# First modulation matrix of a Hyena and DeltaNet trunk layer: 512 KB blocks that also use the weight slots, four quadrants of 256 columns per block

## The chip, the core and the metric

The kernel runs on one core of a Trainium2 chip. The metric is the device time of one execution in microseconds (us), as the median of the runs shown; smaller is better. Everything is float32 in memory. Products with large weights are made of three matmuls on split operands (a rounded high part and the rest).

## What is computed

One trunk layer acts on 128 context tokens and 256 latent tokens (T = 384) of width D = 2048. It consists of a half-step SwiGLU, a mixer (Hyena long convolutions beside a gated DeltaNet) and a second half-step SwiGLU. Each of the three is normalised before and after and modulated by shift, scale and gate vectors, which come out of a product of two conditioning vectors with the matrix `ada_w` (2048 x 18432). What the opening needs of it:

```python
def adaln(x, g, shift, scale):
    return rms_norm(x, g) * (1.0 + scale) + shift
...
    mod_ctx = (silu(c_ctx)[None] @ ada_w[l] + ada_b[l]).reshape(1, 1, N_MOD, D_MODEL)
    mod_lat = (silu(c) @ ada_w[l] + ada_b[l]).reshape(n_lat_req, 1, N_MOD, D_MODEL)
...
    h = adaln(x, norm_pre[0], mod[:, :, 0], mod[:, :, 1])
    x = x + 0.5 * mod[:, :, 2] * rms_norm(swiglu(h, ffn_wg[0], ffn_wu[0], ffn_wd[0]), norm_post[0])
```

So before the first large product can run, the first 4096 columns of `ada_w` (32 MB; shift and scale of the first sub-layer) have to be multiplied with two vectors, the tokens normalised, and `h` made. Beside this the kernel computes in its opening the spectra of the Hyena's long filters, which depend on the filter weights alone.

## The kernel before

A scheduler sets the order of the instructions on each engine when the program is built; each engine then runs its list in order, and waits where an instruction needs something that is not there yet. An instruction that waits holds up all behind it on its engine, and this includes DMA issues.

`run` (from line 1209) starts with an opening of some 150 us, which is written as two interleaved strands:

- `first_mods` (line 282) goes in two halves g over 16 row blocks kt of the matrix. Each step loads 1 MB of `ada_w` (L296, tile `aw`, three buffers, issued on SP's queue) and multiplies it on TensorE (PE) with the two conditioning vectors: four matmuls of 32 x 512 (L302), one for each quadrant of 32 columns of the array, into one PSUM bank `ada`. After each half come a copy (L307, ScalarE, called ACT), four transposes (L310) and the sums that give `modT` and `ab`. `modulate` then makes 8 of the 16 slices k of `h` (L431 on VectorE, called DVE; L433 on ACT), its rounded part `hh` (L123, ACT) and the rest `hl` (L124, here on GpSimd, called POOL).
- The generator `work` is advanced once per step. It holds the Hyena filters (`filters`) and, in `tokens`, the token work. The filters go through four turns, one for each order and half of the channels: matmuls L715/L716, windowed taps `fh` (L718), their sums in `slot` (L723/L724), absolute values `fab` (L726 to L728), norms (L733/L735), transforms by matmul (L745, L753), their copies and sums `fev` (L746, L754, L756, L757), and six stores `spec` of 256 KB to DRAM per turn (L740, issued on ACT's queue). The token work stands after the first turn: transposes of the tokens (L267, with L270 or L277), the squares (L406, ACT) with their sums on PE (L408), the root (L410 to L416), its spread (L445) and a copy of it (L1253).

`hl` lies in the buffer that `slot` held, so that the first write of `hl` comes after the last L753 that reads `slot`.

What follows, from the first `ffn` on, is dense work on PE: `unit` (line 128) loads 512 KB of weights (L142, SP), rounds them (`hi`, L123, ACT) and forms the rest (`lo`, L124, DVE), with three buffers each of `raw`, `hi` and `lo` of 512 KB in a pool `wp` of their own; `mm3` runs L149 to L151. `self.gate` holds the first weight loads back until some named instructions are done: the load of step kt = 12 of the first half, and two of the filters.

The DMA issues of SP and ACT together take eight completion semaphores (DMAHW0 to DMAHW7 in the orders below) in turn, in the scheduler's order; a load that takes one waits until the earlier load on it has landed.

Of the kernel before, what the change touches and what calls it, by code (L numbers as in the profile page):

```python
# [11 lines left out]
F32 = mybir.dt.float32  # L12
# [7 lines left out]
P = 128  # L20
D = 2048
KT = D // P
# [6 lines left out]
DH = 1024  # L29
# [76 lines left out]
class Builder:  # L106
# [175 lines left out]
    def first_mods(self, pool, x, hh, hl, work):  # L282

        nc = self.nc
        w = self.I["ada_w"][0][:, :2 * D].rearrange("r (m c) -> r m c", m=2)
        ab = pool.tile([P, 2, KT], F32, name="ab0")
        pre = self.vec["pre"]
        rb = None  # L290
        asb = self.early(512)
        for g in range(2):
            pa = self.psm.tile([P, 512], F32, tag="mm", name="ada")
            for kt in range(KT):
                aw = pool.tile([P, 2, DH], F32, tag="aw", name="aw", bufs=3)
                load = nc.sync.dma_start(out=aw, in_=w[kt * P:kt * P + P, :, g * DH:g * DH + DH])  # L296
                if g == 0 and kt == 12:
                    self.gate.append(load.ins)
                for m in range(2):
                    for h in range(2):  # L300
                        q = 32 * (2 * m + h)
                        nc.tensor.matmul(pa[q:q + 32, :], self.cs[:, kt, :], aw[:, m, h * 512:h * 512 + 512],  # L302
                                         start=kt == 0, stop=kt == KT - 1)
                got = next(work, None)
                rb = got if got is not None else rb
            sb = asb
            nc.scalar.copy(out=sb, in_=pa)  # L307
            pt = self.aux()
            for k in range(4):
                nc.tensor.transpose(pt[:, k * P:k * P + P], sb[:, k * P:k * P + P], self.ident)  # L310
            src = pt.rearrange("p (k m h v) -> p m h k v", k=4, m=2, h=2)
            gs = slice(8 * g, 8 * g + 8)
            b = self.vec["adab"][:, :2 * KT].rearrange("p (m t) -> p m t", m=2)[:, :, gs].rearrange("p m (h k) -> p m h k", h=2)
            for v in range(2):
                dst = self.modT[:, 0:2, v, gs].rearrange("p m (h k) -> p m h k", h=2)
                nc.vector.tensor_tensor(out=dst, in0=src[:, :, :, :, v], in1=b, op=ALU.add)
                nc.vector.scalar_tensor_tensor(out=ab[:, v, gs], in0=self.modT[:, 1, v, gs], scalar=1.0, in1=pre[:, gs],
                                               op0=ALU.add, op1=ALU.mult)
            for k in range(8 * g, 8 * g + 8):
                self.modulate(pool, 0, k, ab, x, rb, hh, hl, nc.gpsimd)  # L320
# [1060 lines left out]
```

## Time and profile before

| | us |
|---|---|
| median of 3 runs (lowest, highest) | 3302.22 (3301.97, 3307.99) |
| the profiled execution | 3302.25 |
| its span, first to last instruction | 3300.5 |
| PE busy in the span | 3200.0 (97%) |
| VectorE busy | 2091.5 (63%) |
| ScalarE busy | 1091.9 (33%) |
| GpSimd busy | 194.8 (6%) |
| mean granted TensorE clock, share of full speed | 0.987 |

The profile is of one execution. Its span is 1.75 us shorter than the time of the same execution, and that time lies within 0.03 us of the median. Times in rows count from the span's start. An engine is busy while an instruction runs on it; "idle before" and the waits name what released it. Rows with a q behind the engine (SPq, ACTq) are the DMA issues of that engine.

### The profile page before, as it was taken

What the parts mean: (1) busy time and instruction counts of PE and PEld (TensorE: products, weight loads), DVE (VectorE), ACT (ScalarE), POOL (GpSimd) and SP (SyncE); (2) the same over time, 40 slices, a digit from 0 to 9 for tenths busy, and PEclk for the clock granted to TensorE, in tenths of its full rate; (3) what the DMA queues carried; (4) which work ended last, traced back from release to release, by engine and by line L of the source; (5) the groups of instructions that cost most, each with busy time, mean ns of one, the idle gap of its engine ahead of it and who ended that gap; (6) DMA issues with size and microseconds to landing.
All of it is one profiled execution on the core that took longest, in us unless ns stands there. A gap on an engine that the chain in (4) does not pass through costs nothing.

```text
span 3300.5 us, 43912 instructions
## 1 busy us (share of the span) xinstructions
PE 3200.0 (97%) x17485; PEld 2915.9 (88%) x17485; DVE 2091.5 (63%) x2838; ACT 1091.9 (33%) x1583; POOL 194.8 (6%) x225
## 2 busy tenths in 40 slices
PE   6899999999999997999999999989999999999998
PEld 2499999899999996999999998879899999999996
DVE  4579889797979646677656665489444334444335
ACT  3442222222222235333333333353222222222223
POOL 1110000000000002000122320020000000000001
PEclk9899999999999998999999999989999999999999
DMA  9877767676868543433422234448343344333343
GB/s 331 281 264 253 235 224 249 211 240 218 258 211 257 166 153 126 140 125 114 123 75 67 77 96 160 131 142 264 122 150 125 128 128 126 124 127 125 125 130 113
DMA packets 362356, 554.03 MB, mean 168 GB/s; under 512 B 19876, under 2 KB 264970, under 8 KB 360360
## 3 DMA queue, kind: packets, MB, share of 16 engines
q1 hardware_dynamic: 351272, 527.59, 49.5%
q0 software_dynamic: 2800, 12.32, 1.1%
q10 hardware_dynamic: 8080, 11.33, 1.0%
q8 instruction: 137, 2.24, 0.3%
q14 instruction: 67, 0.55, 0.0%
HBM read 535.91 MB, written 15.25 MB: 167 GB/s over the span
## 4 chain that ended last, share of the span: by engine, by line
PE 88%; DVE 6%; DMA 3%; issue 2%; POOL 1%; ACT 1%; DVEq 0%; ACTq 0%; SPq 0%; POOLq 0%
PE mm L151 18%; PE mm L149 18%; PE mm L150 18%; PE mt L559 8%; PE mt L557 8%; PE mt L558 8%; DMA aw<-in_ada_w_dram 2%; DVE acc L339 1%; PE pb L1095 1%; PE pb L1090 1%; DVE lo L124 1%; PE aux L1137 1%; PE aux L1161 1%; PE ada L302 1%; PE pa L346 1%
## 5 line engine op out<-in xcount | busy, mean ns | idle before, releaser
L124 DVE TENSOR_TENSOR lo<-raw,hi 128x1024 fp32r<-128x1024 f32 (+1 forms) x676 | 823.6, 1220 | 714.6 <-ACT hi L123 712.9
L123 ACT CAST hi<-raw 128x1024 fp32r<-128x1024 f32 (+1 forms) x676 | 707.2, 1047 | 1616.9 <-PE mm L150 958.0
L150 PE MATMUL mm<-hl,hi 128*128 128x384 f32 x2320 | 779.6, 336 | 0.1
L149 PE MATMUL mm<-hh,hi 128*128 128x384 f32 x2320 | 776.4, 337 | 1.3 <-DVE hx L770 1.0
L151 PE MATMUL mm<-hh,lo 128*128 128x384 f32 x2320 | 765.1, 337 | 0.0
L339 DVE SCALAR_TENSOR_TENSOR acc<-aw,cs,acc 128x1024 f32<-128x1024 f32 x420 | 520.1, 1280 | 25.5 <-DMA aw<-in_ada_w_dram 24.5
L150 PE MATMUL mm<-yl,hi 128*128 128x384 f32 x1408 | 470.4, 334 | 0.0
L149 PE MATMUL mm<-yh,hi 128*128 128x384 f32 x1408 | 468.7, 334 | 0.7 <-ACT yh L123 0.7
L151 PE MATMUL mm<-yh,lo 128*128 128x384 f32 x1408 | 465.7, 334 | 1.4 <-DVE lo L124 1.4
L149 PEld LDWEIGHTS mm<-hh,hi 128*128 128x128 f32 x2320 | 434.1, 187 | 7.7 <-ACT hi L123 3.2
L150 PEld LDWEIGHTS mm<-hl,hi 128*128 128x128 f32 x2320 | 434.5, 187 | 6.9 <-issue 4.0
L151 PEld LDWEIGHTS mm<-hh,lo 128*128 128x128 f32 x2320 | 432.9, 187 | 8.0 <-issue 5.6
L558 PE MATMUL mt<-hi,gl 128*128 128x512 f32 x1056 | 414.1, 392 | 0.0
L557 PE MATMUL mt<-hi,gh 128*128 128x512 f32 x1056 | 413.5, 392 | 0.1
L559 PE MATMUL mt<-lo,gh 128*128 128x512 f32 x1056 | 398.8, 394 | 1.4 <-DVE lo L124 1.4
L149 PEld LDWEIGHTS mm<-yh,hi 128*128 128x128 f32 x1408 | 264.1, 188 | 1.5 <-ACT yh L123 1.1
L151 PEld LDWEIGHTS mm<-yh,lo 128*128 128x128 f32 x1408 | 263.9, 188 | 1.7 <-DVE lo L124 1.7
L150 PEld LDWEIGHTS mm<-yl,hi 128*128 128x128 f32 x1408 | 264.3, 188 | 0.4
L557 PEld LDWEIGHTS mt<-hi,gh 128*128 128x128 f32 x1056 | 198.2, 188 | 48.2 <-issue 3.4
L559 PEld LDWEIGHTS mt<-lo,gh 128*128 128x128 f32 x1056 | 198.2, 188 | 47.5 <-DVE lo L124 2.6
L558 PEld LDWEIGHTS mt<-hi,gl 128*128 128x128 f32 x1056 | 198.3, 188 | 44.6
L582 DVE TENSOR_TENSOR yacc<-mt,yacc 128x512 f32<-128x512 f32 x216 | 145.1, 687 | 145.1 <-PE mt L559 144.4
(344 smaller groups left out, 2455.5 us busy)
## 6 DMA issues: line engine op xcount, KB each, us to landing
aw<-in_ada_w_dram SPq DMA_DIRECT2D x224, 512.0 KB, 4.4
raw<-in_ffn_wg_dram SPq DMA_DIRECT2D x176, 512.0 KB, 3.8
raw<-in_ffn_wu_dram SPq DMA_DIRECT2D x176, 512.0 KB, 4.4
raw<-in_ffn_wd_dram SPq DMA_DIRECT2D x176, 512.0 KB, 3.5
raw<-in_w_in_dram SPq DMA_DIRECT2D x112, 512.0 KB, 3.6
aw<-in_ada_w_dram SPq DMA_DIRECT2D x32, 1024.0 KB, 8.2
raw<-in_w_out_dram SPq DMA_DIRECT2D x32, 512.0 KB, 3.7
spec<-fev ACTq DMA_DIRECT2D x24, 256.0 KB, 5.9
```

Of the source, the lines that this page charges most:

```text
L123: self.nc.scalar.copy(out=hi, in_=src)
L124: return (eng or self.nc.vector).tensor_tensor(out=lo, in0=src, in1=hi, op=ALU.subtract)
L149: t.matmul(out, hi[:, k, c], xh, start=first, stop=False)
L150: t.matmul(out, hi[:, k, c], xl, start=False, stop=False)
L151: t.matmul(out, lo[:, k, c], xh, start=False, stop=last)
L302: nc.tensor.matmul(pa[q:q + 32, :], self.cs[:, kt, :], aw[:, m, h * 512:h * 512 + 512], start=kt == 0, stop=kt == KT - 1)
L339: nc.vector.scalar_tensor_tensor(out=d, in0=aw, scalar=self.cs[:, kt, v:v + 1], in1=d, op0=ALU.mult, op1=ALU.add)
L346: nc.tensor.matmul(pa[32 * q:32 * q + 32, :], self.pick[:, v], acc[:, v, q * 512:q * 512 + 512], start=v == 0, stop=v == 1)
L557: mm(pts[t], xh[:, ts], hi[:, k], start=first, stop=False)
L558: mm(pts[t], xl[:, ts], hi[:, k], start=False, stop=False)
L559: mm(pts[t], xh[:, ts], lo[:, k], start=False, stop=last)
L582: nc.vector.tensor_tensor(out=y, in0=pt, in1=y, op=ALU.add)
```

## The change

The matrix comes in 64 blocks of 512 KB (one half m of the columns at a time) instead of 32 of 1 MB. Of every five of the first 46 blocks three take a slot of the pool `wp` (one of the nine of `raw`, `hi` and `lo`, in turn), the other two and all later ones take one of six buffers of their own (3 MB, as much as before). So up to 15 blocks can be ahead, then six. Each block is multiplied by four matmuls of 32 x 256, one per quadrant, and each m has a PSUM bank of its own; two copies bring both banks together, and the views of the transposed result are written for the new layout. The gate for the first sub-layer weights moves from the load of the 13th MB to that of block 52 (the 53rd, in the 27th MB).

```diff
+        spare = itertools.cycle(("raw", "hi", "lo"))
+        def block(i, src):
+            if i < 46 and i % 5 > 1:
+                aw = self.wp.tile([P, DH], F32, tag=next(spare), name="aw", bufs=3)
+            else:
+                aw = pool.tile([P, DH], F32, tag="aw", name="aw", bufs=6)
+            load = nc.sync.dma_start(out=aw, in_=src)
+            if i == 52:
+                self.gate.append(load.ins)
+            return aw
         for g in range(2):
-            pa = self.psm.tile([P, 512], F32, tag="mm", name="ada")
+            pa = [self.psm.tile([P, 512], F32, tag="mm", name="ada")[:, :256] for m in range(2)]
             for kt in range(KT):
-                aw = pool.tile([P, 2, DH], F32, tag="aw", name="aw", bufs=3)
-                load = nc.sync.dma_start(out=aw, in_=w[kt * P:kt * P + P, :, g * DH:g * DH + DH])
-                if g == 0 and kt == 12:
-                    self.gate.append(load.ins)
+                aw = [block((g * KT + kt) * 2 + m, w[kt * P:kt * P + P, m, g * DH:g * DH + DH]) for m in range(2)]
                 for m in range(2):
-                    for h in range(2):
-                        q = 32 * (2 * m + h)
-                        nc.tensor.matmul(pa[q:q + 32, :], self.cs[:, kt, :], aw[:, m, h * 512:h * 512 + 512],
-                                         start=kt == 0, stop=kt == KT - 1)
+                    for q in range(4):
+                        nc.tensor.matmul(pa[m][32 * q:32 * q + 32], self.cs[:, kt, :],
+                                         aw[m][:, q * 256:q * 256 + 256], start=kt == 0, stop=kt == KT - 1)
                 got = next(work, None)
                 rb = got if got is not None else rb
             sb = asb
-            nc.scalar.copy(out=sb, in_=pa)
+            for m in range(2):
+                nc.scalar.copy(out=sb[:, m * 256:m * 256 + 256], in_=pa[m])
```

In the kernel after, lines from `block` on are ten higher: the loads are L300, the block matmuls L311, the copies L317, the transposes L320, the squares L416, the stores `spec` L750, the last transforms L763; L142 and L149 to L151 keep their numbers. The scheduler sets a new order, and three places of it matter below.

First, ACT around the token work. Before, the four later stores of turn 0 stand ahead of the copies of the transposed tokens, and wait for semaphores of early loads and stores:

```order
L740 DMA spec<-fev 128x2x256 [waits DMAHW3_49,DVE_49]
L740 DMA spec<-fev 128x2x256 [waits DMAHW5_49]
L740 DMA spec<-fev 128x2x256 [waits DMAHW7_49,DVE_49]
L740 DMA spec<-fev 128x2x256 [waits DMAHW0_49]
L270 COPY x<-aux 128x4x128 [waits PE_49] x4
L406 ACTIVATE early<-x 128x384 [waits DVE_49,Activation_49]
```

After, on ACT:

```order
L270 COPY x<-aux 128x4x128 [waits PE_49] x4
L750 DMA spec<-fev 128x2x256 [waits DMAHW3_49,DVE_49]
L750 DMA spec<-fev 128x2x256 [waits DMAHW4_49]
L750 DMA spec<-fev 128x2x256 [waits DMAHW6_49,DVE_49]
L750 DMA spec<-fev 128x2x256 [waits DMAHW7_49]
L416 ACTIVATE early<-x 128x384 [waits DVE_49,Activation_49]
```

The stores now stand right ahead of the first square, and the semaphores that they take belong to blocks of the matrix. Which, SP's order shows, here blocks 33 to 41 (the first block is 0), on which the eight semaphores go round with the gaps that ACT's stores take:

```order
L300 DMA aw<-in_ada_w_dram 128x1024 [waits DMAHW4_49,PE_49]
L300 DMA aw<-in_ada_w_dram 128x1024 [waits DMAHW5_49,PE_49]
L300 DMA aw<-in_ada_w_dram 128x1024 [waits DMAHW6_49,PE_49]
L300 DMA aw<-in_ada_w_dram 128x1024 [waits DMAHW7_49,PE_49]
L300 DMA aw<-in_ada_w_dram 128x1024 [waits DMAHW0_49,PE_49]
L300 DMA aw<-in_ada_w_dram 128x1024 [waits DMAHW1_49,PE_49]
L300 DMA aw<-in_ada_w_dram 128x1024 [waits DMAHW2_49,PE_49]
L300 DMA aw<-in_ada_w_dram 128x1024 [waits DMAHW5_49,PE_49]
L300 DMA aw<-in_ada_w_dram 128x1024 [waits DMAHW0_49,PE_49]
```

Between the seventh and the ninth of these rows the stores took DMAHW3 and 4, then 6 and 7; the loads last on those are blocks 32, 33, 35 and 36.

Second, ACT in turn 2 of the filters. Before, from the absolute values of its first third to the first transform copy, with the rounding of the first weights (`hi`) long done in turn 1:

```order
L726 ACTIVATE fab<-fh 128x512 [waits DVE_49]
L701 CAST wf<-w_616 128x512 [waits DMASW2_49,DMASW1_49,PE_49]
L701 CAST wf<-w_616 128x512
L710 ACTIVATE win<-slot,tn 128x512 [waits DVE_49]
L746 COPY fev<-aux 128x512 [waits DMAHW5_49,DMAHW6_49,DMAHW1_49,PE_49]
```

After, in the same stretch:

```order
L736 ACTIVATE fab<-fh 128x512 [waits DVE_49]
L123 CAST hi<-raw 128x1024 [waits DMAHW6_49]
L711 CAST wf<-w_713 128x512 [waits DMASW2_49,DMASW1_49,PE_49]
L711 CAST wf<-w_713 128x512
L123 CAST hi<-raw 128x1024 [waits DMAHW0_49]
L123 CAST hh<-h 128x384 [waits Activation_49]
L720 ACTIVATE win<-slot,tn 128x512 [waits DVE_49]
L123 CAST hh<-h 128x384 [waits Activation_49]
L123 CAST hi<-raw 128x1024 [waits DMAHW0_49]
```

The three casts of the first weights moved one turn later, and each waits for its load.

Third, PE at the end of the opening. Before, the last blocks stand between and behind the last transforms; two more and the transposes L310 follow inside the stream of products:

```order
L753 MATMUL aux<-slot,early 128x512 [waits Activation_49]
L302 MATMUL ada<-aw,cs 32x512 [waits DMAHW5_49]
L302 MATMUL ada<-aw,cs 32x512 x3
L753 MATMUL aux<-slot,early 128x512 [waits DVE_49]
L302 MATMUL ada<-aw,cs 32x512 [waits DMAHW6_49]
L302 MATMUL ada<-aw,cs 32x512 x3
L150 MATMUL mm<-hl,hi 128x384 [waits Pool_49]
```

After:

```order
L763 MATMUL aux<-slot,early 128x512 [waits Activation_49] x2
L763 MATMUL aux<-slot,early 128x512 [waits DVE_49]
L320 MATMUL aux<-base,early 128x128 [waits Activation_49]
L320 MATMUL aux<-base,early 128x128 x3
L150 MATMUL mm<-hl,hi 128x384 [waits Pool_49]
```

All 64 blocks now stand ahead of the last transforms, and no block stands in the stream of products. Counted on PE's list, 14 blocks (7 MB) stand up to the end of turn 0 where 5 MB stood before, 35 (17.5 MB) up to the root of the tokens (12 MB before), 47 (23.5 MB) up to the end of turn 1 (17 MB), and 60 (30 MB) up to the end of turn 2 (23 MB).

## Rows read from the trace of the kernel before

**Rows 1.** Busy time of the engines: us, share of the span, instructions.

```profile
PE 3200.0 (97%) x17485; PEld 2915.9 (88%) x17485; DVE 2091.5 (63%) x2838; ACT 1091.9 (33%) x1583; POOL 194.8 (6%) x225
```

**Rows 2.** Stretches: length; PE, PEld, DVE, ACT, POOL busy (instructions); granted clock, DMA share, GB/s.

```profile
0.00:10.00 10.00, 1.79 (x3) 0.46 (x3) 1.95 (x9) 1.62 (x3) 6.46 (x18) 1.00 0.77 204
10.00:35.00 25.00, 13.37 (x40) 4.55 (x40) 14.24 (x26) 10.76 (x15) 3.37 (x6) 0.92 1.03 381
35.00:50.00 15.00, 14.62 (x54) 6.13 (x58) 6.50 (x11) 5.57 (x10) 1.17 (x2) 0.68 0.72 229
55.00:60.00 5.00, 4.49 (x40) 3.12 (x36) 3.68 (x6) 1.10 (x3) 0.00 (x0) 1.00 0.97 353
60.00:80.00 20.00, 16.84 (x110) 6.98 (x102) 8.06 (x14) 11.25 (x21) 1.41 (x2) 1.00 1.04 406
150.00:700.00 550.00, 549.51 (x2988) 513.92 (x2985) 468.22 (x470) 174.94 (x218) 17.92 (x16) 1.00 0.73 237
```

**Rows 3.** SP's queue, 0 to 200 us, waits: us in total, times, longest.

```profile
SPq L296 <- PE ada L302: 76.7, 22, 9.3
```

**Rows 4.** Other engines' waits, 0 to 185 us: us in total, times, longest.

```profile
ACT early L639 <- DMA aw<-in_ada_w_dram: 11.4, 1, 11.4
...
PE ada L302 <- DMA aw<-in_ada_w_dram: 6.9, 4, 2.5
```

**Rows 5.** Timeline, single instructions of the opening: start, duration, instruction, idle before.

```profile
15.26 0.34 ACTq L259 DMA_DIRECT2D early<-in_pos_dram  x1
...
50.83 0.37 ACTq L740 DMA_DIRECT2D spec<-fev  x1
...
59.48 0.52 ACT L406 ACTIVATE early<-x 128x384 f32<-128x384 f32 x1 [3.03 <-DVE x L277]
...
68.86 0.52 ACT L406 ACTIVATE early<-x 128x384 f32<-128x384 f32 x1 [0.38 <-PE sums L408]
...
76.09 0.68 DVE L718 SCALAR_TENSOR_TENSOR fh<-win,aux 128x512 f32<-128x512 f32 x1
...
100.28 0.69 DVE L718 SCALAR_TENSOR_TENSOR fh<-win,aux 128x512 f32<-128x512 f32 x1 [3.28 <-PE aux L716]
...
126.56 0.69 DVE L718 SCALAR_TENSOR_TENSOR fh<-win,aux 128x512 f32<-128x512 f32 x1 [6.91 <-PE aux L716]
...
141.02 1.07 ACT L746 COPY fev<-aux 128x512 f32<-128x512 f32 x2 [3.66 <-DMA spec<-fev]
...
145.97 0.59 ACT L754 COPY fev<-aux 128x512 f32<-128x512 f32 x1 [3.35 <-DMA spec<-fev]
```

**Rows 6.** Chain of the work that ended last, 0 to 170 us: start, us, what.

```profile
3.46 11.78 DMA aw<-in_ada_w_dram
...
76.77 1.13 DVE lo L124
...
78.50 2.27 DVE lo L124 x2
...
84.05 1.87 PE ada L302 x8
```

**Rows 7.** DMA issues, 60 to 80 us: count, KB each, median us to landing.

```profile
aw<-in_ada_w_dram SPq DMA_DIRECT2D x5, 1024.0 KB, 8.2
raw<-in_ffn_wg_dram SPq DMA_DIRECT2D x3, 512.0 KB, 6.0
raw<-in_ffn_wu_dram SPq DMA_DIRECT2D x2, 512.0 KB, 7.5
```

**Rows 8.** Timeline of POOL and PE from 150 us: the end of the opening.

```profile
151.47 3.25 POOL L124 TENSOR_TENSOR hl<-h,hh 128x384 fp32r<-128x384 f32 x3 [16.92 <-PE aux L753]
...
152.52 0.44 PE L150 MATMUL mm<-hl,hi 128*128 128x384 f32 x1
...
154.80 1.06 PE L302 MATMUL ada<-aw,cs 128*32 128x512 f32 x8
...
166.18 0.60 PE L310 MATMUL aux<-base,early 128*128 128x128 f32 x4
```

More of the change, by code (lines that the diff above doesn't have):

```diff
@@ L310, in first_mods @@
                 nc.tensor.transpose(pt[:, k * P:k * P + P], sb[:, k * P:k * P + P], self.ident)
-            src = pt.rearrange("p (k m h v) -> p m h k v", k=4, m=2, h=2)
+            src = pt.rearrange("p (m k q v) -> p m q k v", m=2, k=2, q=4)
             gs = slice(8 * g, 8 * g + 8)
-            b = self.vec["adab"][:, :2 * KT].rearrange("p (m t) -> p m t", m=2)[:, :, gs].rearrange("p m (h k) -> p m h k", h=2)
+            b = self.vec["adab"][:, :2 * KT].rearrange("p (m t) -> p m t", m=2)[:, :, gs].rearrange("p m (q k) -> p m q k", q=4)
             for v in range(2):
-                dst = self.modT[:, 0:2, v, gs].rearrange("p m (h k) -> p m h k", h=2)
+                dst = self.modT[:, 0:2, v, gs].rearrange("p m (q k) -> p m q k", q=4)
                 nc.vector.tensor_tensor(out=dst, in0=src[:, :, :, :, v], in1=b, op=ALU.add)
```

## The prediction, made before the change was run

> **What bounds the kernel now.** I read the shares of busy time first: PE is busy 97% of the span [rows 1]. Then the table of stretches: from 150 us on PE is busy 549.51 of 550 us [rows 2], so a microsecond won or lost before the stream of products passes to the end one to one, and the change can only act through the moment at which that stream starts. That is the opening, where PE is not the bound. What ends it is the row of POOL at 151.47: the first `hl` waited 16.92 us for the last transform L753, and the first product behind it runs at 152.52 [rows 8]. So the end of the filters sets the start, not the end of the matrix; I follow the filters back. Their turns 1, 2 and 3 begin with the `fh` at 76.09, 100.28 and 126.56 [rows 5]: 24.2, 26.3 and 24.9 us. Ahead of turn 1 stands the token work, with its first square at 59.48 [rows 5], 16.6 us before turn 1.
>
> Second, the supply of the matrix. SP held its loads 76.7 us for PE to free one of three buffers [rows 3], and the rate fell to 229 GB/s in 35 to 50 us [rows 2]. More slots will fill this gap. But PE itself waited for a block only 6.9 us in all, in four waits [rows 4], so a full queue is worth little directly. The chain does pass through a load once early: ACT stood 11.4 us [rows 4] behind its own issue at 15.26 [rows 5], which began when the load of 3.46 + 11.78 = 15.24 landed [rows 6]. That row shows what matters below: a DMA issue on ACT that takes a semaphore of a block still under way stops ACT, and all behind it, until that block has landed.
>
> **The change part by part.** *Same bytes, same columns.* 64 x 4 matmuls of 256 columns stream as many columns as 32 x 4 of 512. One MB of blocks (eight records for its four matmuls) takes 1.06 us [rows 8], and 1.87 where the clock was down [rows 6]; per MB I keep these. The extra copies and issues stand on ACT and SP beside other work: nothing.
>
> *The wait on ACT.* The four stores of turn 0 now stand right ahead of the first square and wait for blocks 32, 33, 35 and 36. Before, they waited for early loads, and were issued at 50.83, as soon as the data were there [rows 5]. So the squares cannot start before 37 blocks have landed. By then the queues have moved 37 x 0.524 = 19.4 MB of blocks and, from the sizes in the code, 7.4 MB more (tokens 3.15, filter weights 1.57, decay 1.05, stores 0.52, the rest 1.1): 26.8 MB. The first 10 us moved 204 GB/s x 10 = 2.0 MB [rows 2]. The other 24.8 MB at 0.39 MB/us (between the 381 of 10 to 35 us, the full queue with these small loads in it, and the 406 of 60 to 80 us [rows 2]) take 64 us: block 36 lands at 74 (71 by 406; 80 by the 353 of 55 to 60 us [rows 2]). Against 59.48 that is 14.5 us later. It covers another loss: with the semaphores moved, ACT's load of `fwd` waits for the first token load, so that turn 0 ends perhaps 6 us later, at 57; by 74 this is over.
>
> *From the squares to turn 1.* 16.6 us before. PE had blocks between the squares, and the squares waited for copies of the tokens; after, tokens and most blocks are ready when ACT is released. 16 squares at 0.52 are 8.3; from the end of the last square (68.86 + 0.52) to turn 1 it was 6.7 [rows 5], with 0.9 of a block in it: 5.8. Together 14. Turn 1 starts at 74 + 14 = 88, against 76.1.
>
> *Turn 1.* The three `lo` on the chain, 1.13 + 2.27 = 3.4 us [rows 6], move to turn 2; one MB more of blocks (6 against 5) costs 1.1 to 1.9 us [rows 6, 8]. 24.2 - 3.4 + 1.2 = 22; it ends at 110.
>
> *Turn 2.* It takes up the three `lo` (3.4) and three `hi`, half a MB more of blocks (0.6), and stores on ACT that wait for blocks or weights issued late in turn 1, as at 15.26 (0 to 4; I take 2, since by then the queue is no longer behind); PE's waits for blocks go (up to 2.5 each [rows 4]). 26.3 + 3.4 + 0.6 + 2 - 2 = 30. Bounds: nothing, if the splits fall into idle time of DVE (26), and 34. It ends at 140.
>
> *Turn 3.* Before, ACT waited 3.66 + 3.35 = 7.0 us for stores to land [rows 5] while blocks were loading beside them. With the last block landed before this turn they land sooner: 24.9 - 7.0 = 17.9 at best, and I give 2 back for the DVE work that those waits hid. 20, at most 21: the filters end at 160, against 151.5.
>
> *The stream.* The transposes (0.60) now stand ahead of the first product, which comes at 160 + 1.05 + 0.6 = 161.7. Before it came at 152.52, but two rounds of blocks (1.06 each) and the transposes (0.60) were still to do inside the stream [rows 8]: 155.2 in the same coin. The difference is +6.5 us.
>
> *The weights.* The gate falls one turn later, and `wp` is busy with blocks. The first weights are needed at 160; at 7.5 us from issue to landing [rows 7] and one `lo` they are there. The fourth waits for a `lo` of turn 2 and has a turn to land. Nothing, and up to 3 us if they are late.
>
> **The sum.** 3302.25 + 6.5 = 3309 us; the profiled execution lies 0.03 us from the median, so no correction. With all terms at their low ends (71, 26, 18) it is 3300, with all at their high ends (80, 34, 21) 3320; the forecast's own range is 3300 to 3317.
>
> **A rule that speaks against the change.** The rows show 406 GB/s over 20 us in which five loads of 1 MB and five of 512 KB were mixed [rows 2, 7], so the smaller size by itself does not slow a full queue. The Trainium skill, "DMA: Bandwidth & Descriptors", section Bandwidth, says to batch transfers to at least 1 MiB to reach three quarters of the peak, and has 341 GB/s for 1 MB alone. By that rate, as an estimate from the page, block 36 would land at 10 + 24.8/0.341 = 83, nine later than I take it, and the kernel would take 3318. The rows, with several in flight, speak against it; rival D is the same worry at the lowest rate of a refill in the rows.
>
> **Rivals.** (B) *The wait costs little.* If the blocks land at the top rate and the turns lose the waits named above without taking up the splits in full, we get 71 + 14 = 85, turns of 22, 26.3 and 18.5, an end at 151.8 and a first product at 153.4, against 155.2: -1.8, that is 3300; anything from 3296 to 3308 looks like this. For it: DVE and ACT are idle a good part of each turn. Against it: the chain of [rows 6] showed the splits on it in turn 1.
>
> (C) *The supply was the true bound* (faster). If the squares start at 64, because the semaphores come free in another way than I read it (or because the tokens are late by the extra blocks alone), turn 1 starts at 78, and with every wait for a block or a store gone the turns take 20.8, 24 and 18: the end is at 140.8, the first product at 142.4, -12.8, hence 3289.5. It decides if block 36 lands before 66. For it: SP's 76.7 us of waits, and 6.91 and 3.28 us of DVE waits for PE at the start of turns 3 and 2 [rows 5], where blocks stood ahead. Against it: at 66 us only 2.0 + 56 x 0.406 = 24.7 MB can have come at the highest rate of the table, and 26.8 are needed.
>
> (D) *The supply is slower than I take it* (slower by more). If the 512 KB blocks, each waiting for PE in its slot and for its semaphore, run at 353 [rows 2] as in the refill at 55 to 60 us, block 36 lands at 80, turn 1 starts at 94, turn 2 takes 32: +14, 3316. It decides if slots come free late around 55 to 60, since block 36 takes the buffer of block 21, which PE reaches only behind turn 0.
>
> (E) *The change doesn't do what it says:* the queue runs no further ahead because a load waits for the load eight places before it. Then 8 x 0.5 MB are in flight, and that already fills the queue; the rate stays and the result is the forecast or B.
>
> **How the numbers follow.** Chances: forecast 0.40, half of it above the bound of 0.2% (6.6 us, about what a measurement of this kernel can tell from no change); B and E 0.17; C 0.24; D 0.19. Slower is 0.20 + 0.19 = 0.39, same 0.20 + 0.17 = 0.37, faster 0.24. The likeliest is 3309. The range has to reach to C, or it would leave out more than 2 in 10, and to most of D: 3290 to 3318. The forecast's own range is 3300 to 3317.
>
> **What would show it.** In the profile after: the rate of 35 to 50 us near 400 GB/s; a wait of ACT at a store ahead of L416 and the first square at 74 (70 to 80); the first `fh` of turn 1 at 88, of turn 2 at 110, of turn 3 at 140; three `lo` in turn 2; no wait of ACT for stores in turn 3; the last L763 at 160, and a product right behind it. It would be wrong if the first square came before 66, if PE waited in the stream of products for `lo`, or if the turns kept their length although the loads are gone from them.

## The result and the profile after

The change makes the kernel slower: 3322.68 us (median; 3322.45 to 3327.7) against 3302.09, a ratio of 1.0062 with a 95% interval of 1.0045 to 1.0079, or 20.6 us. The forecast was 3309 with a range of 3290 to 3318: the sign is right, the forecast loss of some 7 us is a third of the measured one, and the time lies above the range. The profiled execution took 3322.64, with a span of 3320.8.

What the change was to bring to the queue, it brought. The stretches after (columns as in [rows 2]):

```profile
10.00:75.00 65.00, 41.87 (x322) 18.86 (x318) 27.74 (x54) 20.93 (x30) 4.01 (x7) 0.99 1.03 394
...
35.00:50.00 15.00, 10.76 (x82) 5.64 (x82) 8.62 (x14) 7.35 (x12) 0.52 (x1) 1.00 1.03 417
...
150.00:160.00 10.00, 6.74 (x21) 3.12 (x20) 9.04 (x15) 3.50 (x7) 0.77 (x2) 0.64 0.29 99
160.00:170.00 10.00, 10.00 (x33) 5.44 (x32) 3.31 (x6) 2.95 (x5) 0.00 (x0) 0.68 0.18 59
```

The hole of 35 to 50 us is filled (417 GB/s, 229 in [rows 2]), and 394 GB/s over 10 to 75 us is what the sum had assumed (390). SP's waits changed their kind: instead of 76.7 us for PE [rows 3] it now waits 33.4 us for PE and 51.6 us for the landing of earlier blocks.

```profile
SPq L300 <- DMA aw<-in_ada_w_dram: 51.6, 33, 4.1
...
SPq L300 <- PE ada L311: 33.4, 15, 8.7
```

And yet all that follows is later. The timeline after, with the rows that answer to [rows 5] and [rows 8] (start, duration, instruction, idle before):

```profile
21.08 0.52 ACT L649 ACTIVATE early<-early 64x384 f32<-64x384 f32 x1 [16.34 <-DMA xtok<-in_x_prompt_dram]
...
69.59 5.56 ACTq L750 DMA_DIRECT2D spec<-fev  x4
75.58 1.35 ACT L416 ACTIVATE early<-x 128x384 f32<-128x384 f32 x3 [11.55 <-DMA aw<-in_ada_w_dram]
...
92.00 1.27 DVE L728 SCALAR_TENSOR_TENSOR fh<-win,aux 128x512 f32<-128x512 f32 x2
...
116.30 0.69 DVE L728 SCALAR_TENSOR_TENSOR fh<-win,aux 128x512 f32<-128x512 f32 x1 [5.75 <-PE aux L726]
...
147.40 0.69 DVE L728 SCALAR_TENSOR_TENSOR fh<-win,aux 128x512 f32<-128x512 f32 x1 [3.60 <-PE aux L726]
...
170.37 2.96 POOL L124 TENSOR_TENSOR hl<-h,hh 128x384 fp32r<-128x384 f32 x3 [15.61 <-PE aux L763]
...
171.41 0.45 PE L150 MATMUL mm<-hl,hi 128*128 128x384 f32 x1 [0.70 <-POOL hl L124]
```

The row of 75.58 is the predicted one: ACT stood 11.55 us, released by a block, behind four stores on its own list. Not all of that is wait for blocks: the last sums that the stores send were done at 68.45. The four stores then went out between 69.59 and 74.79, the last one as block 36 landed (74.77). The first product runs at 171.41 instead of 152.52, 18.9 us later, and the span is 20.3 us longer. So nearly all of the loss is made before the stream, and most of it before turn 1 (92.0 against 76.1). Open is how much of it the stores made.

### The profile page after: what moved, and what is told of

It is laid out like the page before. It is cut to its first block, busy times and chain, and to the rows that moved or that the text cites. A ratio compares the mean times of both kernels' runs of the same rounds, so it can differ in the third digit from the quotient of the medians.

```text
span 3320.8 us, 44472 instructions
## 1 busy us (share of the span) xinstructions
PE 3206.1 (97%) x17741; PEld 2924.7 (88%) x17741; DVE 2090.8 (63%) x2838; ACT 1094.7 (33%) x1587; POOL 195.0 (6%) x225
## 4 chain that ended last, share of the span: by engine, by line
PE 88%; DVE 6%; DMA 3%; issue 2%; ACT 1%; POOL 1%; ACTq 0%; DVEq 0%; POOLq 0%
PE mm L151 18%; PE mm L149 18%; PE mm L150 18%; PE mt L569 8%; PE mt L567 8%; PE mt L568 8%; DMA aw<-in_ada_w_dram 2%; DVE acc L349 1%; PE pb L1105 1%; PE pb L1100 1%; DVE lo L124 1%; PE aux L1147 1%; PE aux L1171 1%; PE pa L356 1%; PE aux L763 1%
## 5 line engine op out<-in xcount | busy, mean ns | idle before, releaser
L149 PE MATMUL mm<-hh,hi 128*128 128x384 f32 x2320 | 777.2, 337 | 1.3 <-DVE hx L780 1.0
L151 PE MATMUL mm<-hh,lo 128*128 128x384 f32 x2320 | 766.3, 337 | 1.1 <-DVE lo L124 1.0
L349 DVE SCALAR_TENSOR_TENSOR acc<-aw,cs,acc 128x1024 f32<-128x1024 f32 x420 | 519.8, 1277 | 27.1 <-DMA aw<-in_ada_w_dram 26.4
L149 PE MATMUL mm<-yh,hi 128*128 128x384 f32 x1408 | 468.7, 334 | 0.9 <-ACT yh L123 0.9
L151 PE MATMUL mm<-yh,lo 128*128 128x384 f32 x1408 | 465.8, 334 | 1.7 <-DVE lo L124 1.6
L149 PEld LDWEIGHTS mm<-hh,hi 128*128 128x128 f32 x2320 | 434.4, 187 | 8.2 <-ACT hi L123 2.5
L151 PEld LDWEIGHTS mm<-hh,lo 128*128 128x128 f32 x2320 | 432.7, 187 | 9.6 <-issue 5.6
L151 PEld LDWEIGHTS mm<-yh,lo 128*128 128x128 f32 x1408 | 263.7, 188 | 2.3 <-DVE lo L124 2.3
L149 PEld LDWEIGHTS mm<-yh,hi 128*128 128x128 f32 x1408 | 264.0, 188 | 1.5 <-ACT yh L123 1.1
```

What stands on the lines that cost most here:

```text
L149: t.matmul(out, hi[:, k, c], xh, start=first, stop=False)
L151: t.matmul(out, lo[:, k, c], xh, start=False, stop=last)
L349: nc.vector.scalar_tensor_tensor(out=d, in0=aw, scalar=self.cs[:, kt, v:v + 1], in1=d, op0=ALU.mult, op1=ALU.add)
```

## The experiments

All runs are in one table; each ratio is to runs of the kernel before that were made beside it. "Spread" is the start of the six matmuls L455 (L445 before) that end the token work; times in the columns behind the first two are from one profiled execution each, which can lie some 3 us from the median of its kernel (5 in e9), so that differences of 1 or 2 us in a single stretch show nothing by themselves.

| run | time (median), us | ratio to before, 95% interval | turn 0 starts | first square | spread | first product |
|---|---|---|---|---|---|---|
| before | 3302.1 | | 27.1 | 59.5 | 73.1 | 152.5 |
| after | 3322.7 | 1.0062 [1.0045, 1.0079] | 32.9 | 75.6 | 89.0 | 171.4 |
| e1 stores on GpSimd | 3320.2 | 1.0051 [1.0036, 1.0066] | 32.8 | 75.4 | 87.9 | 168.8 |
| e2 no spare slots | 3310.3 | 1.0022 [1.0011, 1.0033] | 33.5 | 67.2 | 78.6 | 160.0 |
| e3 quadrants alone | 3303.6 | 1.0006 [0.9997, 1.0015] | 25.9 | 59.4 | 71.9 | 154.2 |
| e4 gate as before | 3320.5 | 1.0055 [1.004, 1.007] | 33.3 | 78.3 | 91.1 | 172.9 |
| e5 stores behind squares | 3312.9 | 1.0038 [1.0024, 1.0052] | 32.6 | 71.6 | 83.8 | 162.7 |
| e6 blocks behind spread | 3325.0 | 1.0077 [1.006, 1.0094] | 33.4 | 76.5 | 87.8 | 174.2 |
| e7 both | 3324.1 | 1.0075 [1.0058, 1.0092] | 33.1 | 71.4 | 82.9 | 171.5 |
| e8 before, tokens earlier | 3303.3 | 1.0004 [0.9994, 1.0013] | 27.4 | 44.3 | 57.3 | 155.6 |
| e9 early loads on GpSimd | 3326.3 | 1.0076 [1.0061, 1.0091] | 28.8 | 79.0 | 96.3 | 177.9 |
| e10 e9 and e5 together | 3321.9 | 1.0056 [1.0041, 1.0071] | 30.2 | 79.2 | 94.6 | 172.8 |
| e11 before, early loads on GpSimd | 3304.4 | 1.0005 [0.9996, 1.0015] | 27.4 | 58.3 | 71.3 | 151.2 |
| e12 halved loads, 3 buffers | 3308.4 | 1.0023 [1.0014, 1.0033] | 32.6 | 67.6 | 79.2 | 160.6 |
| e13 halved from the 6th MB on | 3304.8 | 1.0007 [0.9998, 1.0017] | 27.9 | 63.7 | 75.6 | 152.1 |
| e14 e2, stores behind squares | 3312.1 | 1.0032 [1.0019, 1.0045] | 33.1 | 67.5 | 79.8 | 161.3 |
| e15 e5, sums first | 3314.3 | 1.0039 [1.0024, 1.0054] | 33.2 | 71.2 | 84.4 | 167.1 |
| e16 sums first | 3325.5 | 1.007 [1.0053, 1.0087] | 32.5 | 77.2 | 90.0 | 175.6 |

**The parts of the change (e1 to e4).** Four kernels, each with one piece undone or alone. e1 moves the stores off ACT:

```diff
-                    nc.scalar.dma_start(out=self.spec[o, half * 2 + qq, :, slot], in_=ev[:, :, qq * 256:qq * 256 + 256])
+                    nc.gpsimd.dma_start(out=self.spec[o, half * 2 + qq, :, slot], in_=ev[:, :, qq * 256:qq * 256 + 256])
```

> The kernel after, with the filter spectra's stores issued on GpSimd's queue instead of ScalarE's, so that ScalarE issues nothing that waits for a block of the matrix. Theory 1 (the stores ahead of the first square stop ScalarE until block 36 has landed, and this delay is passed to the end): ScalarE's wait of 11.6 us at L416 is gone, the first square comes at 64 to 67 us instead of 75.6, the spread L455 some 9 us earlier (80 instead of 89), and the time falls by 8 to 12 us to 3311 to 3315. Theory 2 (it is the order on TensorE: 35 blocks instead of 24 half-MB blocks stand ahead of the spread, and they land no sooner): the squares start early but stretch until block 34 has landed at 72 to 75, the later turns still wait for blocks, and the time falls by less than 5 us, to 3318 or more.

Measured 3320.18; in e1's timeline ACT no longer waits for a block, and the first square is where it was:

```profile
75.38 1.35 ACT L416 ACTIVATE early<-x 128x384 f32<-128x384 f32 x3 [7.15 <-DVE x L277]
```

By the numbers theory 2 was nearer. But the run is not clean: the scheduler moved more than the stores, and PE's transforms of turn 0 ran at a lower clock (35 to 60 us: 0.80 here, 1.00 after), so that the token work began at 63.0 instead of 58.8. It needed a kernel in which nothing but the stores moves (e5).

e2 takes the spare slots away:

```diff
-            if i < 46 and i % 5 > 1:
+            if i < 0:
```

> The kernel after without the nine spare slots: 512 KB blocks in six buffers of their own (3 MB, as in the kernel before), the rest as after. On TensorE's list 28 blocks instead of 35 stand ahead of the spread, and the stores of turn 0 stand ahead of the token copies again and wait for blocks up to about the 20th. Theory 1 (deeper prefetch moved blocks and stores ahead of the token work) expects a first square near 64 us and 3305 to 3312. Theory 2 (blocks on TensorE's list, at the rate at which they come) expects about half of the loss, 3310 to 3315, since six slots supply 28 blocks later than fifteen do. If the block size itself costs (each load pays its issue and landing twice), the rate in 10 to 75 us is below that of before and the time is 3322 or more.

Measured 3310.26, where the two ranges overlap, with the first square at 67.2 and the spread at 78.6. The spare slots make 12.4 of the 20.6 us; 512 KB blocks in six buffers of their own, with the gate and the quadrants, make 8.

e3 keeps 1 MB loads and three buffers, and has only the new layout (two banks, 256 columns):

```diff
-                    for h in range(2):
-                        q = 32 * (2 * m + h)
-                        nc.tensor.matmul(pa[q:q + 32, :], self.cs[:, kt, :], aw[:, m, h * 512:h * 512 + 512],
...
+                    for q in range(4):
+                        nc.tensor.matmul(pa[m][32 * q:32 * q + 32], self.cs[:, kt, :], aw[:, m, q * 256:q * 256 + 256],
...
```

> The kernel before with only the new layout: 1 MB loads in three buffers and the gate as before, but two PSUM banks and four quadrants of 256 columns per half. The first product's list has about 25 half-MB groups ahead of the spread, as before (24). Both theories expect the time of before within 0.1%, 3300 to 3306, with the first square at 59 to 61 us. If the shorter matmuls cost TensorE's time or clock, the loss would be here: 3308 or more.

Measured 3303.55, no difference that can be told from none: the quadrants are not the loss.

e4 puts the gate back:

```diff
-            if i == 52:
+            if i == 24:
```

> The kernel after with the gate of the first sub-layer weights at block 24 (the 13th MB, as in the kernel before) instead of block 52. The delay up to the spread at 89 us stays in either theory, and so most of the loss. If the late weights cost turn 2 its 31.1 us (three casts and three splits inside it and stores that wait for late loads), turn 2 falls to about 28 and the time to 3318 to 3320; if they cost nothing there, 3322 to 3324.

Measured 3320.5, with turn 2 at 28.1 us (120.0 to 148.2) instead of 31.1, but turn 1 at 25.9 instead of 24.3, and a spread two us later in this execution. The sum moves by 2 us at most.

**The stores and the blocks apart (e5 to e7), and the token work earlier (e8).** e5 puts the four later stores of turn 0 behind the last square on ACT's list, e6 puts the blocks that are written behind the token work also behind the spread on PE's list, and e7 does both; `issue_after` only orders instructions of one engine.

```diff
+            if i == 0:
+                yield
+            with ExitStack() as st:
+                if i == 0:
+                    st.enter_context(self.tc.issue_after(self.sqi))
+                put(0, lo)
+                put(1, hi)
...
+                        if rb is not None:
+                            st.enter_context(self.tc.issue_after(self.rbi))
                         for q in range(4):
```

> The kernel after, with the four later stores of turn 0 put behind the last square on ScalarE's list; TensorE's list is unchanged up to the spread (35 blocks ahead of it). In the run with the stores on GpSimd the first square came no earlier (75.38), but there turn 0 also ended later, at a lower clock. Theory 1 (ScalarE's wait for block 36 is what delays the squares): the first square comes at 66 to 69, the spread at 79 to 82, the time is 3311 to 3314. Theory 2 (the 35 blocks between the token work's instructions on TensorE's list set the spread): the squares begin earlier but are drawn out, the spread stays at 85 to 89 and the time at 3317 to 3322.

> The kernel after, with every block that is written behind the token work also placed behind the spread on TensorE's list: 20 blocks instead of 35 stand ahead of it, the other 15 move into turn 1. The four stores still stand ahead of the squares, but wait for blocks 27 to 30 (landing near 66 by 10 us + 21.9 MB at 0.39). Theory 2 (blocks on the list) expects the first square at 66 to 68, squares without blocks between them (10 us less), the spread at 76 to 79, and 3305 to 3311. Theory 1 expects a gain from the earlier block alone: the spread at 79 to 82 and 3311 to 3315. If the blocks only pass their time on to turn 1 (25 there instead of 12, at 0.5 to 1 us each), turn 1 grows by 7 to 13 us and the time stays above 3315.

> Both at once: stores behind the last square and the later blocks behind the spread (20 ahead). If both causes are real and add up, the first square comes at 62 to 65, the spread at 73 to 76 (before: 73.1), and the time is that of before within 4 us, 3300 to 3307. If only the stores count, it equals the run with the stores moved alone; if only the blocks count, the run with the blocks moved alone.

e5 measured 3312.91, 9.8 us less than after: in time what theory 1 expected, but the first square comes at 71.6, not at 66 to 69, and the spread at 83.8. ACT in e5:

```profile
71.61 1.35 ACT L416 ACTIVATE early<-x 128x384 f32<-128x384 f32 x3 [6.52 <-DVE x L277]
...
79.70 2.32 ACTq L750 DMA_DIRECT2D spec<-fev  x4
```

The stores ahead of the squares are a cause, shown here, and about half of the loss. Behind them stood something else that would have held the squares until 71.6 anyway: the tokens were not there (DVE x). The trace of the kernel after says the same: the fifth token addition L277, which the square of e5 follows by 0.1 us, ended there at 70.45, 5.1 us ahead of the square.

In e6 the first square comes at 76.5, but not because of the stores: they were all out by 73.7, and the square comes 0.4 us behind the fifth token addition. The transposes had begun late (63.5), behind a turn 0 at a lower clock (35 to 60 us: 0.80). The time is 3325.01. In e7 square and spread are those of e5, without the blocks between, and the time is 3324.13, that of e6 and 11 us above e5. So to take the 15 blocks from ahead of the spread brings it forward by less than a microsecond, and the gain that theory 2 expected is not there. What they cost ahead of the first square is not separated by this, since PE ran at a lower clock in e7 just then (four transposes L267 took 1.12 us, in e5 0.66); from the first square to the spread, with the clock at 1.00 in both, it is 11.6 us without them and 12.2 with them. Put behind the spread, they cost: turn 1 takes 28.0 us (23.5 in e5), turn 2 32.8 (29.3). The granted clock shows with it; first stretches of e7, then of e5 (columns as in [rows 2]):

```profile
60.00:80.00 20.00, 17.13 (x76) 9.84 (x76) 6.63 (x11) 9.04 (x20) 0.00 (x0) 0.74 0.52 196
120.00:140.00 20.00, 12.83 (x63) 5.23 (x64) 11.19 (x15) 14.12 (x25) 0.52 (x1) 0.66 0.99 366
```

```profile
35.00:50.00 15.00, 12.35 (x75) 6.46 (x74) 8.25 (x14) 7.09 (x12) 0.51 (x1) 0.77 1.03 416
60.00:80.00 20.00, 18.23 (x174) 9.41 (x173) 7.45 (x12) 9.98 (x22) 0.00 (x0) 1.00 1.02 389
120.00:140.00 20.00, 19.43 (x114) 8.58 (x113) 10.20 (x15) 8.59 (x15) 0.00 (x0) 0.75 0.82 283
```

e8 goes back to the kernel before and writes the token work after the second third of turn 0 (`itertools.islice(filters, 2)` for 5).

> The kernel before with the token work written after the second third of turn 0 instead of behind turn 0; everything else as before. On TensorE's list 10 MB instead of 12 stand ahead of the spread, 13 MB at the start of turn 1 (12). If the time from the spread on is what counts (rest of turn 0 then still ahead of turn 1), nothing is won: the spread comes near 62, turn 1 starts near 76 as before, and the time is 3299 to 3305. If the token work is on the chain by itself and turn 0's end can hide behind it, turn 1 starts near 70 and the time is 3294 to 3298.

Measured 3303.26, no change, as in the first case: the spread comes 16 us earlier, at 57.3, but the rest of turn 0 then stands between it and turn 1, which starts at 72.8 instead of 76.1, and more than the three us is lost again in turn 1 (30.1 us, 24.2 before).

**The late turn 0 (e9 to e13).** In the kernels above that start with 512 KB blocks turn 0 starts 5 to 6 us late, because ACT waits for the first token load before its first filter instruction (row of 21.08 above; 11.4 us in [rows 4], 16.3 after). e9 issues the loads of tokens, positions and `fwd` on GpSimd's queue in the kernel after, e10 in e5, e11 in the kernel before:

```diff
-            nc.scalar.dma_start(out=xt[:, t], in_=src)
+            nc.gpsimd.dma_start(out=xt[:, t], in_=src)
...
-        nc.scalar.dma_start(out=fwd, in_=I["fwd"].rearrange("p (t f) -> p t f", t=3))
+        nc.gpsimd.dma_start(out=fwd, in_=I["fwd"].rearrange("p (t f) -> p t f", t=3))
```

> The kernel after, with the loads of the tokens, of the position table and of the transform matrix issued on GpSimd's queue, so that ScalarE no longer waits 16 us for a semaphore before its first filter instruction. Turn 0 should start near 27 us instead of 32.9 (27.1 before). The four stores still stand ahead of the squares and wait for blocks of about the same place. If they decide (as the prediction had it: the late turn 0 is covered by them), the first square stays at 73 to 76 and the time at 3319 to 3323. If the late turn 0 adds to the loss by itself, square, spread and time come 4 to 6 us earlier, 3315 to 3318.

> The same loads on GpSimd's queue, and the four stores behind the last square (which alone gave a first square at 71.6, a spread at 83.8 and 3312.9). If the late turn 0 is the second cause, the first square comes at 65 to 67, the spread at 77 to 79, and the time is 3306 to 3309. If the blocks and sums that stand between the token work's instructions decide, the first square stays at 69 to 72 and the time at 3311 to 3314.

> The kernel before with those loads on GpSimd's queue: ScalarE's wait of 11.4 us at its first filter instruction goes. Turn 0 then starts near 22 to 24 instead of 27.1. If the token work and the turns behind it follow, all comes 3 to 5 us earlier and the time is 3297 to 3300, a version better than both; if the supply of the matrix sets the spread (13 MB ahead of it), it stays at 72 to 74 and the time at 3301 to 3304.

Turn 0 started earlier by 4.1 us in e9 and 2.4 in e10, not at all in e11 (27.4), and nothing came of it: 3326.27 and 3321.91, both above every range that I had given, and 3304.44. In e9 the first square even moved back to 79.0; 37 instead of 35 blocks stand ahead of the spread there, and PE waited for them:

```profile
PE ada L311 <- DMA aw<-in_ada_w_dram: 12.0, 8, 3.3
```

(2.9 us in four waits in the kernel after.) The edit changed the order of too much, so that it says nothing on the late turn 0. e12 and e13 are cleaner (the diff is that of e13; e12 has the last two lines for all loads): quadrants, buffers and gate as in e3, but the 1 MB loads halved, in e12 all of them, in e13 from the sixth on, so that the semaphores at the early loads are those of before.

```diff
+                if g == 0 and kt < 5:
                     load = nc.sync.dma_start(out=aw, in_=w[kt * P:kt * P + P, :, g * DH:g * DH + DH])
+                else:
+                  for m in range(2):
+                    load = nc.sync.dma_start(out=aw[:, m], in_=w[kt * P:kt * P + P, m, g * DH:g * DH + DH])
```

> The kernel with the four quadrants of 256 columns, three buffers of 1 MB and the gate as before, in which only the loads are halved: two of 512 KB into each buffer. The load of the transform matrix then waits for the first token load again and turn 0 starts near 32 us (27.1 before, 25.9 with 1 MB loads); on TensorE's list 26 blocks stand ahead of the spread (25 with 1 MB loads). If the late turn 0 costs by itself: spread at 76 to 79, 3306 to 3310. If it is covered by the supply of the matrix: spread at 71 to 74, 3301 to 3305. If six separate buffers and the later gate made the loss: also 3301 to 3305, but with turn 0 late.

> As the run before, but the first five MB come in 1 MB loads, so that the semaphores at the load of the transform matrix are those of the kernel before; 25 blocks stand ahead of the spread. Turn 0 starts at 26 to 28. If the late turn 0 is the cause: the spread comes at 71 to 74 and the time is 3301 to 3305, 4 to 6 us less than the run before. If halved loads cost in another way (landing, issue, order): the same time as the run before within 2 us.

Measured 3308.39 and 3304.75. ACT's first filter instruction, in e12 and in e13:

```profile
20.73 0.52 ACT L640 ACTIVATE early<-early 64x384 f32<-64x384 f32 x1 [15.98 <-DMA xtok<-in_x_prompt_dram]
```

```profile
16.89 0.52 ACT L643 ACTIVATE early<-early 64x384 f32<-64x384 f32 x1 [12.16 <-DMA slot<-in_hy_decay_dram]
```

Turn 0 starts 4.7 us apart, the first squares are 3.9 apart, the spreads 3.6, the medians 3.6. So a late turn 0 is passed on, where nothing later covers it. The intervals of the two runs just overlap, so the size is good to two or three us; the two profiled executions are 8.5 us apart at the first product, since turn 3 took 25.4 us in e12 at a mean clock of 0.80 and 19.5 in e13 at 1.00. It is the halved loads at the start that make the wait: six buffers and the later gate add nothing that can be told from none (e12 3308.4, e2 3310.3).

**What is left (e14 to e16).** e14 takes the stores out of the version without spare slots.

> The version without spare slots (3310.3, spread at 78.6) with the four stores of turn 0 behind the last square. There the stores stand ahead of the token copies and wait for blocks that have landed by then, so that moving them should win little: spread at 76 to 79, 3307 to 3311. If they cost there as much as with the spare slots (5 us at the spread), it comes at 73 to 75 and the time is 3301 to 3305.

Measured 3312.09, spread at 79.8: no gain in time. The reason that the expectation gave is wrong, though: in e2 ACT does wait at its stores for a block, and the token copies with it.

```profile
60.94 2.05 ACT L270 COPY x<-aux 128x512 f32<-128x512 f32 x4 [8.77 <-DMA aw<-in_ada_w_dram]
```

From the first transpose to the first square e2 takes 9.7 us and e14 7.9; but e14's transposes began 2.2 us later (59.6), behind a turn 0 that ended at a lower clock. The four kernels together say what the depth costs: with the stores ahead of the squares the spare slots make 12.4 us (3322.7 against 3310.3), with the stores behind them 0.8 (e5 3312.9, e14 3312.1). So nearly all of what the spare slots cost hangs on the place of these four stores; each of the differences is good to some 5 us.

In e5 the token work still takes 11.8 us from the first transpose (59.8) to the first square, against 6.8 before (52.7 to 59.5). In the traces the first transposes each wait for ACT's copy of the one before, while the last sums of turn 0 stand behind the first token addition on DVE's list. e15 and e16 put these sums first, with and without the stores moved:

```diff
+                with self.tc.issue_after(self.fevi):
                     nc.vector.tensor_tensor(out=dst.rearrange("p k (r c) -> p k r c", c=GRID_W),
...
```

> The kernel after with the four stores behind the last square and, besides, the last sums of turn 0 (L766, L767) ahead of all token additions on VectorE's list. If those sums, which hold PSUM buffers, draw the transposes out, the first square comes at 66 to 68 instead of 71.6, the spread at 78 to 80, and the time is 3306 to 3310 (3312.9 without this). If it is the blocks between the transposes (29 ahead of the first square), square and time stay within 1.5 us of 71.6 and 3312.9.

> The kernel after with only those sums ahead of the token additions. The stores still wait for block 36 ahead of the squares. If block 36 decides, the first square stays at 74 to 76 and the time at 3319 to 3323, though the transposes end earlier.

Measured 3314.28 and 3325.46 (above its range), with first squares at 71.2 and 77.2: the sums are not the reason, or for no more than 1 us. The pair is also the edit of e5 a second time, on another order: the stores behind the squares win 11.2 us here, 9.8 there. Blocks between the first transposes do not space them out either: in e5 the first groups of four start at 59.82, 61.15 and 62.49 with a block between each, in e7 at 58.73, 60.06 and 61.39 without one, each time behind ACT's copy of the group before. So it stays open what draws the transposes out by these 4 to 5 us.

Put in a row, from before to after by one piece at a time, the 20.6 us are: the quadrants 1.5 (e3, not to be told from none), the halved loads 4.8 (e12), six buffers and the later gate 1.9 (e2, not to be told from none either), the spare slots 12.4 (after).

## Why the prediction fell short

*The bound and the place: right.* The stream passes a later start on one to one, as forecast: over all eighteen kernels the span less the first product's start lies between 3145.8 and 3152.1 us, while that start moves by 27. The matrix was not the bound: a full queue brought nothing.

*The step that failed: the relief.* In four stretches the forecast took 12.4 us off: from the squares to turn 1 (16.6 to 14), turn 1 (24.2 to 22), turn 3 (24.9 to 20) and the stream (2.7). The runs gave back 0.6: these took 16.4, 24.3 and 23.0 us, and the stream 1.4 more.

*The wait on ACT: right in place and time, wrong in worth.* Block 36 landed at 74.8 (74 forecast), and the squares began at 75.6. But the prediction gave the whole 14.5 us to it and held that it covered the late turn 0. That the time of the first square came out right is partly luck: two delays lay over one another. e5 shows that without the stores the square would come at 71.6: 4 us at the first square are theirs (9.8 us in time; in e5 the turns up to `hl` are shorter too, 74.9 us against 78.4, for which the runs show no reason), the other 12 come from the late start of turn 0 (5.5), the drawn-out transposes (5) and some 2 between. The covered loss was real and would have stood behind.

*From the squares to turn 1: 16.4 us, not 14.* The step credited that blocks and tokens would be ready. They were, and the squares still took from 75.6 to 85.4. PE ran at first at a lower clock (0.85 us for an L418 at 76.16, 0.49 later): from the first square to the spread it was 13.4 us here, 12.2 in e5 with as many blocks between at full clock, and 11.6 in e7 without blocks.

*Turn 1: 24.3, not 22.* The three splits left it, as the order said, and it was no shorter. In [rows 6] they stood on the chain; taken away, another wait took their place (DVE waited 5.75 us for PE's L726 at its end, the row of 116.30; before 3.28 [rows 5]).

*Turn 2: 31.1 (30 forecast).* Right: splits and casts moved in, and ACT waited again for blocks ahead of its stores (3.6 us at 126.6).

*Turn 3: 23.0, not 20.* The 7.0 us of waits for stores [rows 5] did go. But PE ran the end of the turn at a lower clock, with no blocks left beside it: 0.64 and 0.68 over 150 to 170 us. The same four matmul records of the transforms, before and then after:

```profile
136.97 1.13 PE L745 MATMUL aux<-slot,early 128*128 128x512 f32 x2
138.18 1.13 PE L745 MATMUL aux<-slot,early 128*128 128x512 f32 x2
```

```profile
158.47 2.05 PE L755 MATMUL aux<-slot,early 128*128 128x512 f32 x2
160.61 2.06 PE L755 MATMUL aux<-slot,early 128*128 128x512 f32 x2
```

That is 1.8 us for these four alone. I had looked at what the turn waits for, not at PE's clock. That the missing blocks lowered it is not shown (e12 had 0.80 over this turn with 12 blocks in it).

*The stream: the credit of 2.7 us did not come.* The two rounds of blocks and the transposes did leave it, but PE met new small waits there: the rows of L149 to L151 and of the products behind them have 3.4 us more idle time in sum (for `hl` 0.6, for `lo` of the first products 1.1, the rest in pieces of under 0.8). As the stream's length differs by up to 6 us among the eighteen executions, this step is within their scatter.

The sum closes: 6.5 forecast, plus 1.6 (square), 2.4, 2.3, 1.1 and 3.0 (the steps above), less 0.7 (first product right behind `hl`), plus 4.1 in the stream (2.7 credited and 1.4 more) gives 20.3, the difference of the spans; it is of one execution each. The loss that I named was there; most of the relief that I set against it failed to come. The high ends of my own terms added up to 3320, and the range stopped short of them. Of the rivals D had the nearest time (3316), but for another reason: the supply was as fast as I took it. The Trainium skill, "DMA: Bandwidth & Descriptors", section Bandwidth, asks for transfers of at least 1 MiB for three quarters of the peak, and the prediction's estimate by its rate, 3318, was nearer still. The trace does not bear that reason out for a queue with many transfers in it: 394 GB/s over 65 us with blocks of 512 KB stand beside the 381 and 406 of the full stretches before [rows 2], and block 36 landed at 74.8, not at 83.

## What to carry to other kernels

A DMA issue on a computing engine takes a completion semaphore out of a small common round (eight here); whoever prefetches deeper, or halves the transfers, should look up which loads those semaphores belong to now, and what stands behind the issue on its engine. Here the place of four stores was nearly all that the deeper prefetch cost: 12.4 us with them ahead of the squares, 0.8 with them behind. Set a price on a wait by what would be late next, and give credit for relief off the chain only where a row shows that nothing else is late at the same time. More loads in flight gained nothing here, where the consumer's own chain sets the pace: the queue ran at 394 GB/s and the kernel lost 20 us.

## What the chip showed that I had not expected

- PE's granted clock was lower in some stretches that the blocks had left (e7, 60 to 80 us: 0.74, e5 1.00; after, 150 to 170: 0.64 and 0.68), and in the latter matmuls of the filters took 1.03 us for 0.57. That the missing blocks are the reason is not shown: the clock fell with the blocks in place too (e5, 35 to 50 us: 0.77 at 416 GB/s; after, with the same blocks ahead: 1.00 at 417). A turn of the filters took 19.5 us at a clock of 1.00 (turn 3 of e13) and 25.4 at 0.80 (e12).
- The token, position and transform loads on GpSimd's queue (e9, e10) made the opening longer by 7 to 11 us at the spread than the same kernels with ACT's queue, though ACT was free earlier; in the kernel before (e11) they made no difference. In e9 and e10 PE ran at a lower clock over the transposes (60 to 80 us: 0.74; e5 1.00), and in e9 it waited 12.0 us for blocks. Why was not settled.
